# A fifth MLP pair's first two blocks ahead of the MLP, and three changes of order in layer 1's mixer and projection

## The chip, the cores and the metric

The kernel runs on one core of one Trainium2 chip. The metric is the device time of one execution in microseconds (us). Three runs of the kernel before took 2485.15, 2485.99 and 2488.28 us. A separate execution was profiled; every row shown here is from that one.

## What is computed

Two layers of a decoder trunk over 1024 positions of width 1024, in fp32. Layer 0 mixes with a gated DeltaNet, layer 1 with a state-space scan that ends in a gated linear unit (GLU). Beside the mixer, 4 heads of cross-attention read 256 memory tokens. Both outputs are concatenated (1536 rows), projected, added to the scaled input and normalised; an MLP with squared ReLU follows in the same way.

```
h = jnp.concatenate([mix, cross], axis=-1) @ w_o[i]
x = layer_norm(DN_ALPHA * x + h, ln1_g[i], ln1_b[i])
f = jnp.square(jax.nn.relu(x @ mlp_w1[i])) @ mlp_w2[i]
x = layer_norm(DN_ALPHA * x + f, ln2_g[i], ln2_b[i])
```

In layer 1, the mixer's last step is `out = zg * sigmoid(zg @ w_glu + b_glu)`.

## The kernel before

**Matmuls in three passes.** Every fp32 operand is split into a high part (a ScalarE cast to the type fp32r) and a low part (a VectorE subtraction). `mm3` (lines 386 to 391) multiplies high by high, high by low and low by high into one PSUM bank. Nearly all matmuls of the kernel come from these three lines; the tile's name tells the stage.

**Seven products for eight.** The large products use Strassen's scheme in Winograd's form: two by two blocks, seven block products numbered 1 to 7, and sums of blocks before and after. Product 1 is A11 B11 and product 2 A12 B21; both go to the first quarter of the output. Products 6, 7 and 4 are added onto the bank of product 1 (or 6), and 3 onto that of 5: this is what `onto` says.

**The GLU** (`glu`, lines 2094 to 2206). The weights w and the gated input z lie in SBUF as quarters, four row blocks each. The products go in the order 1, 5, 6, 3, 7, 4, 2, in two sets of four PSUM banks: set 0 (pa, pa, pa, sc) for 1, 6, 7, 4 and set 1 (mm, mm, pi, po) for 5, 3, 2. `sources` makes the sums in place; `t2`, product 4's factor, gets its last subtraction at the start of each of product 4's row blocks. When a product ends, each of its four banks is copied, added or gated by `gate`, which stores rows of the DRAM tensor cat. Product 4 gives rows 0 to 3 of the left half of the tokens, product 2 rows 4 to 7.

**The output projection** (`out_proj`, lines 1639 to 1677, and `out_seven`, lines 1679 to 1767). It has 12 row blocks of 128. Row blocks 8, 9, 10, 11, 0, 1, 2, 3 are paired as (8, 9), (10, 11), (0, 1), (2, 3) for the seven products, so each product loops over four row blocks j. Row block 4 is the fifth one, j = 4: it is added to products 3 and 4, and makes two small products of its own, 8 and 0, of one row block. Product 0 is its part of the output's first quarter, which products 1 and 2 fill. Products 1, 6, 7, 4, 8 are chain 0, and 2, 5, 3, 0 chain 1. In layer 1 chain 0 has the banks (mm, mm, pi, po) and chain 1 (pa, pa, pa, sc), and the order is 2, 1, 5, 6, 7, 4, 3, 8, 0; layer 0 has another order and other banks. After each product four additions on VectorE (lines 1759 and 1761) bring the banks into the rows y. Row blocks 5 to 7 follow as plain products in the tail (`acc_steps`, tile tm, banks pi, po, sc in turn), for one group of 128 positions (tau, 0 to 7) after the other.

**The end of a block** (`block_end`, lines 2390 to 2433). When a tau is complete, `done` normalises its rows, stores them and transposes them. The MLP's input is made into seven factors: "11" and "21" come from tau 0 to 3 alone, "22", "t1", "t2" and "t3" need tau 4 to 7 too, and "n4" comes last, in the four buffers of tag w1.

**Pairs ahead.** The MLP's first product has 16 pairs of hidden blocks, seven products each. Of pairs 0 to 3, products 1 and 2 are done ahead, in `mlp_ahead` (lines 615 to 624): it loads and splits 128x1024 weights (tag raw, two buffers, then tag w1, four), multiplies block 1 into a bank (pA), copies the result away (p1), adds block 2 onto the bank, and stores the first block of the hidden layer. Pairs 0, 1 and 2 are called at tau 5, 6 and 7, pair 3 after tau 7. In `mlp_first` (lines 761 to 772) these pairs do their products 5, 6, 7, 3 and 4 with weights whose sums were made long before (`mlp_weights`, line 642). All other pairs take all seven in `mlp_chain`, with weights summed on the spot (lines 650 to 674). In layer 0, pair 0 begins with ten filler matmuls (line 692) whose result is not used.

**The order.** Nothing runs in program order. `settle` (lines 58 to 293) takes all instructions behind the start-up, gives each a duration from a table (`price`) and a due time from the matmul that needs it, and lists them anew for every engine, DMA issues included. A matmul may be pulled forward by up to 40 us of due time; buffers of one tag are given out in the order of their first uses. The order is fixed at build time; on the chip each engine follows its list and waits where an operand is late.

Of the kernel before, what the change touches and what calls it, by code (L numbers as in the profile page):

```python
# [10 lines left out]
F32 = mybir.dt.float32  # L11
# [5 lines left out]
P = 128  # L17
# [3 lines left out]
HALF = 512  # L21
# [5 lines left out]
def f32(ap):  # L27
    return ap.bitcast(F32)


class Trunk:
# [570 lines left out]
    def hidden_sums(self, n, A11, A12, A21, A22):  # L602
# [7 lines left out]
        for b, o, x, z, op in ((3, A22, A21, A22, ALU.add), (5, A21, A11, A21, ALU.subtract),  # L610
                               (4, A11, A22, A11, ALU.subtract), (6, A12, A12, A11, ALU.subtract)):
            V.tensor_tensor(o, x, z, op=op)
            self.nc.sync.dma_start(self.hd[n, b], o)

    def mlp_ahead(self, i, n, B, ahead):

        w = self.load_split(self.a["w1"][i, 2 * n], "w1", "w1")
        a = self.psum("mm", "pA")
        self.block(a, [z[:, :HALF] for z in w], B["11"], True)
        p1 = self.tile("h3", [P, HALF], F32, "p1")  # L620
        self.nc.scalar.copy(p1, a)
        self.block(a, [z[:, HALF:] for z in w], B["21"], False)
        self.hidden(n, 0, a)
        ahead.append(p1)
# [13 lines left out]
    def mlp_weights(self, i, n, more):  # L638


        V = self.nc.vector
        if not more:
            s3, s1, A22 = (self.tile(t, [P, HALF], F32, "w1s") for t in ("h3", "h5", "h4"))
            self.nc.sync.dma_start(s1, self.wsum[i, n, 1][:, HALF:])
            r = self.load_raw(self.wsum[i, n, 0], "w1s")
            self.nc.sync.dma_start(s3, self.wsum[i, n, 1][:, :HALF])
            self.nc.sync.dma_start(A22, self.a["w1"][i, 2 * n + 1][:, HALF:])
            tags = iter(("h1", "h2") * 5)
            return {m: self.split(x, next(tags), "w" + str(m)) for m, x in ((5, s1), (6, r[:, :HALF]), (7, s3), (3, r[:, HALF:]), (4, A22))}
        r = self.load_raw(self.a["w1"][i, 2 * n], "w1r")  # L650
        A11, A12 = r[:, :HALF], r[:, HALF:]
        A21, A22 = (self.tile("h4", [P, HALF], F32, "w1r") for _ in range(2))
        for c, o in enumerate((A21, A22)):
            self.nc.sync.dma_start(o, self.a["w1"][i, 2 * n + 1][:, c * HALF:(c + 1) * HALF])
        new = lambda nm: self.tile("h3", [P, HALF], F32, nm)

        def sub(o, x, y):
            V.tensor_tensor(o, x, y, op=ALU.subtract)
            return o

        home = {1: 'h1', 2: 'h2', 6: 'h1', 5: 'h2', 7: 'h1', 3: 'h2', 4: 'h2'}
        ops = lambda m, s, nm: self.split(s, home[m], nm)
        s1 = new("s1")
        V.tensor_tensor(s1, A21, A22, op=ALU.add)
        s2 = sub(new("s2"), s1, A11)
        O = {}
        O[1] = ops(1, A11, "a1")
        O[2] = ops(2, A12, "a2")
        O[6] = ops(6, s2, "s2")
        O[5] = ops(5, s1, "s1")  # L670
        O[7] = ops(7, sub(new("s3"), A11, A21), "s3")
        O[3] = ops(3, sub(s2, A12, s2), "s4")
        O[4] = ops(4, A22, "a4")
        return O
# [1004 lines left out]
    def out_seven(self, i, y, early):  # L1679

        nc = self.nc
        V = nc.vector
        tt = lambda o, x, z, op: V.tensor_tensor(o, x, z, op=op)
        A_, S_ = ALU.add, ALU.subtract
        pairs = (8, 9), (10, 11), (0, 1), (2, 3)
        sets = [("mm", "mm", "pa", "pa")] * 2 if early else [("mm", "mm", "pi", "po"), ("pa", "pa", "pa", "sc")]
        w = self.a["w_o"][i]
        row = lambda k: self.cat[k * P:(k + 1) * P]
        L, R = slice(0, HALF), slice(HALF, 2 * HALF)
        tokens = (L, R) if early else (R, L)  # L1690
        ab, rq = [], []
        for c in range(2):
            for o in (ab, rq):
                o.append(self.tile("xT", [P, 8, HALF], F32, "os"))
            for n in range(8):
                p, j = (n % 2, n // 2) if c else (1 - n // 4, n % 4)
                nc.sync.dma_start(ab[-1][:, 4 * p + j], row(pairs[j][p])[:, tokens[c]])
                nc.sync.dma_start(rq[-1][:, 4 * p + j], w[pairs[j][p]][:, (L, R)[c]])
        spare = []

        def sources(m, j):
            if j == 4:
                out = []
                for src, c in ((row(4), tokens[m in (4, 8)]), (w[4], (L, R)[m in (3, 8)])):
                    out.append(self.tile("h3", [P, HALF], F32, "o4"))
                    nc.sync.dma_start(out[-1], src[:, c])
                return out
            aL, bL, aR, bR, rL, qL, rR, qR = (x[h][:, 4 * p + j] for x in (ab, rq) for h in range(2) for p in range(2))
            if m == (6 if early else 5):
                if j % 2 == 0:  # L1710
                    spare.append([self.tile("w1", [P, 2, HALF], F32, "os") for _ in range(2)])
                s1, t2 = (x[:, j % 2] for x in spare[j // 2])
                tt(s1, aR, bR, A_)
                tt(rL, rR, rL, S_)
            elif spare:
                s1, t2 = (x[:, j % 2] for x in spare[j // 2])
            if m == 6:
                tt(aR, aL, aR, S_)
                tt(t2, qR, rL, S_)
                tt(aL, s1, aL, S_)  # L1720
            if m == 7:
                tt(rR, qR, rR, S_)
                tt(bL, bL, aL, S_)
            if m == 4:
                tt(t2, qL, t2, S_)
            return {1: lambda: (aL, rL), 2: lambda: (bL, qL), 6: lambda: (aL, t2), 5: lambda: (s1, rL), 7: lambda: (aR, rR),
                    3: lambda: (bL, qR), 4: lambda: (bR, t2)}[m]()

        def operand(s, tag, nm):
            if isinstance(tag, str):  # L1730
                t = self.tile(tag, [P, 2, HALF], F32R, nm)
                hi, lo = t[:, 0], t[:, 1]
            else:
                hi, lo = (self.tile(t, [P, HALF], F32R, nm) for t in tag)
            nc.scalar.copy(hi, s)  # L1735
            tt(lo, s, f32(hi), S_)
            return hi, lo

        chain = {1: 0, 6: 0, 7: 0, 4: 0, 2: 1, 5: 1, 3: 1, 8: 0, 0: 1}
        into = {1: 0, 6: 1, 2: 0, 7: 3, 5: 3, 4: 2, 3: 1, 8: 3, 0: 0}  # L1740
        held, fresh = {}, {0, 1, 2, 3}
        for m in (2, 1, 6, 7, 4, 5, 3, 8, 0) if early else (2, 1, 5, 6, 7, 4, 3, 8, 0):
            onto = m in (6, 7, 4, 3)
            if not onto:
                held[chain[m]] = [self.psum(t, f"o{m}") for t in sets[chain[m]]]
            bank = held[chain[m]]
            items = {0: (4,), 8: (4,), 3: range(5), 4: range(5)}.get(m, range(4))
            for j in items:
                left, right = sources(m, j)
                h = operand(left, "raw", "ok")  # L1750
                x = operand(right, "w1" if m in (5, 3, 8, 0) else ("h2", "h2"), "ow")
                for t in range(4):
                    c = slice(t * P, (t + 1) * P)
                    self.mm3(bank[t], (h[0][:, c], h[1][:, c]), x, j == items[0] and not onto, j == items[-1], onto)
                    if j == items[-1]:
                        n = into[m]
                        o = y[4 * (n // 2 if early else 1 - n // 2) + t][n % 2]
                        if n in fresh:
                            V.scalar_tensor_tensor(o, o, ALPHA, bank[t], op0=ALU.mult, op1=ALU.add)
                        else:  # L1760
                            tt(o, bank[t], o, A_)
                    yield self.STEP
            fresh.discard(into[m])
            if m == 4:
                yield "early"
            if m == (5 if early else 4):
                yield "late"
# [326 lines left out]
    def glu(self):  # L2094
# [37 lines left out]
        def sources(m, j):  # L2132
# [14 lines left out]
            if m == 3:  # L2147
                tt(s, bL, aL, op=S_)
                tt(rL, qR, rR, op=S_)
            if m == 4:  # L2150
                tt(t2, qL, t2, op=S_)
            return {1: lambda: (aL, rL), 5: lambda: (s, rL), 6: lambda: (aL, t2), 3: lambda: (s, qR),
                    7: lambda: (aR, rL), 4: lambda: (bR, t2), 2: lambda: (bL, qL)}[m]()
# [25 lines left out]

        sets = ("pa", "pa", "pa", "sc"), ("mm", "mm", "pi", "po")  # L2180
        held = {}
        for m in (1, 5, 6, 3, 7, 4, 2):
            own, onto = int(m in (5, 3, 2)), m in (6, 7, 4, 3)
            if not onto:
                held[own] = [self.psum(t, f"g{m}") for t in sets[own]]
# [204 lines left out]
    def block_end(self, i, y, xd):  # L2390
# [3 lines left out]
        B, ahead = {}, []  # L2394

        def done(tau):
# [28 lines left out]
            fill("t3", a)  # L2425
            V.tensor_tensor(c, c, t2, op=ALU.subtract)
            if tau == 7:
                self.mlp_ahead(i, 3, B, ahead)
                B["n4"] = self.x_parts("w1")
                for n in range(4):  # L2430
                    self.parts(as4(y[n][1]), self.x_cols(B["n4"], n))

        return self.out_proj(i, y, done, i == 0), B, ahead

    def mlp_block(self, i, B, ahead, xd, side, out, more):
# [112 lines left out]
```

## Time and profile before

| what | value |
|---|---|
| median of 3 runs | 2485.99 us |
| profiled execution, its own time | 2487.54 us |
| its span, first to last instruction | 2485.8 us |
| TensorE matmuls | 12541, busy 99% of the span |
| VectorE (DVE) | busy 79% |
| ScalarE (ACT) | busy 57% |
| DMA, HBM read and written | 170 GB/s over the span |

In a timeline row stand the start, the duration, the engine, the line, the operation, the tile written and those read, the shape, and in square brackets how long the engine was idle before it and who released it. A matmul's duration of 0.39 us includes its passage through the array; the next starts before it ends. The stretches that matter: layer 0's block end is 741 to 800 us, layer 1's GLU 1640 to 1726, its projection 1726 to 1814, its tail and block end 1814 to 1881, and its pairs from then on.

### The profile page before, as it was taken

What the parts mean: (1) busy time and instruction counts of PE and PEld (TensorE: products, weight loads), DVE (VectorE), ACT (ScalarE), POOL (GpSimd) and SP (SyncE); (2) the same over time, 40 slices, a digit from 0 to 9 for tenths busy, and PEclk for the clock granted to TensorE, in tenths of its full rate; (3) what the DMA queues carried; (4) which work ended last, traced back from release to release, by engine and by line L of the source; (5) the groups of instructions that cost most, each with busy time, mean ns of one, the idle gap of its engine ahead of it and who ended that gap; (6) DMA issues with size and microseconds to landing.
All of it is one profiled execution on the core that took longest, in us unless ns stands there. A gap on an engine that the chain in (4) does not pass through costs nothing.

```text
span 2485.8 us, 37137 instructions
## 1 busy us (share of the span) xinstructions
PE 2452.7 (99%) x12541; PEld 2035.3 (82%) x12541; DVE 1960.5 (79%) x3688; ACT 1404.6 (57%) x3134; POOL 224.8 (9%) x333
## 2 busy tenths in 40 slices
PE   9999999999999999999999999999999999999998
PEld 7888888887787888788888888888877888888886
DVE  7776867685889987879988956698997665588777
ACT  6766767665557576554445244666465555544443
POOL 1111212111001011312220000000010000000001
PEclk9999999999999999999999999999999999999999
DMA  6444445456335665587455488685136544673422
GB/s 205 130 115 147 132 149 148 150 162 199 128 114 184 212 221 191 178 276 248 144 164 158 149 229 237 165 276 194 58 138 229 184 151 153 213 274 99 148 89 98
DMA packets 297807, 425.02 MB, mean 171 GB/s; under 512 B 105312, under 2 KB 141104, under 8 KB 297616
## 3 DMA queue, kind: packets, MB, share of 16 engines
q1 hardware_dynamic: 284912, 392.43, 49.6%
q0 software_dynamic: 10112, 25.64, 3.3%
q10 hardware_dynamic: 2592, 4.59, 0.5%
q8 instruction: 98, 1.61, 0.3%
q14 instruction: 93, 0.76, 0.1%
HBM read 286.79 MB, written 135.76 MB: 170 GB/s over the span
## 4 chain that ended last, share of the span: by engine, by line
PE 85%; DVE 7%; DMA 3%; issue 2%; ACT 2%; SPq 0%; POOL 0%; DVEq 0%; ACTq 0%; POOLq 0%
PE q L389 7%; PE q L390 7%; PE q L391 7%; PE pB L389 4%; PE pB L391 4%; PE pB L390 4%; PE wi L389 3%; PE wi L391 3%; PE wi L390 3%; PE o L389 2%; PE pC L391 2%; PE o L390 2%; PE o L391 2%; PE pC L390 2%; PE pC L389 2%
## 5 line engine op out<-in xcount | busy, mean ns | idle before, releaser
L389 PE MATMUL q<-wkh,hkh 128*128 128x512 f32 x784 | 306.0, 390 | 0.0
L390 PE MATMUL q<-wkl,hkh 128*128 128x512 f32 x784 | 305.7, 390 | 0.0
L391 PE MATMUL q<-wkh,hkl 128*128 128x512 f32 x784 | 305.3, 389 | 0.0
L857 ACT CAST wkh<-wr 128x512 fp32r<-128x512 f32 x168 | 104.8, 624 | 238.7 <-PE q L390 156.9
L389 PEld LDWEIGHTS q<-wkh,hkh 128*128 128x128 f32 x784 | 147.2, 188 | 31.7 <-ACT wkh L857 1.0
L391 PEld LDWEIGHTS q<-wkh,hkl 128*128 128x128 f32 x784 | 147.2, 188 | 30.6
L390 PEld LDWEIGHTS q<-wkl,hkh 128*128 128x128 f32 x784 | 147.2, 188 | 29.9
L858 DVE TENSOR_TENSOR wkl<-wr,wkh 128x512 fp32r<-128x512 f32 x168 | 115.7, 689 | 62.9 <-issue 49.7
L389 PE MATMUL wi<-xTh,wih 128*128 128x512 f32 x376 | 152.3, 405 | 1.8 <-ACT wih L368 1.8
L390 PE MATMUL wi<-xTl,wih 128*128 128x512 f32 x376 | 150.4, 400 | 0.0
L391 PE MATMUL wi<-xTh,wil 128*128 128x512 f32 x376 | 150.2, 400 | 0.0
L512 POOL TENSOR_TENSOR mv<-mv,mhalf 128x1 f32<-128x1 f32 x32 | 31.6, 988 | 1222.9 <-DVE mv L506 1111.1
L858 DVE TENSOR_TENSOR hkl<-hr,hkh 128x512 fp32r<-128x512 f32 x196 | 134.2, 684 | 4.4 <-ACT hkh L857 4.3
L857 ACT CAST hkh<-hr 128x512 fp32r<-128x512 f32 x196 | 120.8, 616 | 4.6 <-DMA hr<-hd 4.6
L389 PE MATMUL o<-ow,ok 128*128 128x512 f32 x256 | 101.4, 396 | 1.0 <-ACT ok L1735 1.0
L391 PE MATMUL o<-ow,ok 128*128 128x512 f32 x256 | 101.4, 396 | 0.1
L390 PE MATMUL o<-ow,ok 128*128 128x512 f32 x256 | 100.1, 391 | 0.1
L850 DVE TENSOR_TENSOR y<-q,y 128x512 f32<-128x512 f32 x136 | 88.0, 682 | 0.0
L389 PEld LDWEIGHTS wi<-xTh,wih 128*128 128x128 f32 x376 | 71.4, 190 | 15.4 <-ACT wih L368 2.0
L391 PEld LDWEIGHTS wi<-xTh,wil 128*128 128x128 f32 x376 | 71.3, 190 | 14.2 <-DVE wil L369 0.8
L390 PEld LDWEIGHTS wi<-xTl,wih 128*128 128x128 f32 x376 | 71.6, 190 | 12.6
L1735 ACT CAST ok<-os 128x512 fp32r<-128x512 f32 x56 | 34.6, 620 | 49.7 <-PE o L391 36.6
(627 smaller groups left out, 7254.2 us busy)
## 6 DMA issues: line engine op xcount, KB each, us to landing
hr<-hd SPq DMA_DIRECT2D x212, 256.0 KB, 2.7
wr<-in_w_dram SPq DMA_DIRECT2D x56, 512.0 KB, 5.7
hd<-u SPq DMA_DIRECT2D x100, 256.0 KB, 2.3
w1r<-in_w_dram SPq DMA_DIRECT2D x48, 512.0 KB, 3.8
hd<-hid SPq DMA_DIRECT2D x60, 256.0 KB, 2.1
hd<-p SPq DMA_DIRECT2D x60, 256.0 KB, 2.3
w1r<-in_w_dram SPq DMA_DIRECT2D x48, 256.0 KB, 3.3
wir<-in_w_in_dram SPq DMA_DIRECT2D x23, 512.0 KB, 3.8
```

Source lines behind the costliest of these rows:

```text
L389: mm(ps, a[0], b[0], start=start, stop=False, skip_group_check=onto)
L390: mm(ps, a[0], b[1], start=False, stop=False, skip_group_check=onto)
L391: mm(ps, a[1], b[0], start=False, stop=stop, skip_group_check=onto)
L512: nc.gpsimd.tensor_tensor(mv[:, 3:4], mv[:, 2:3], self.mhalf[:, 0:1], op=ALU.pow)
L850: V.tensor_tensor(o, bank[t], o, op=ALU.add)
L857: nc.scalar.copy(hi, s)
L858: nc.vector.tensor_tensor(lo, s, f32(hi), op=ALU.subtract)
L1735: nc.scalar.copy(hi, s)
```

## The change

Four edits. A table `AHEAD` says how many pairs are begun ahead in each layer, five in both, and the fifth is called behind the fourth, before "n4"; its copy p1 has a buffer of tag h2 in layer 0 and h5 in layer 1, and pair 4 no longer splits weights 1 and 2 and takes the short form of the pairs ahead. In layer 1's projection product 1 goes before product 2, product 2 gets row block 4 as a fifth one, and product 0 goes. In the GLU, products 4 and 2 change places, and `t2`'s last subtraction moves to product 7.

```
+    AHEAD = (5, 5)
+
     def mlp_ahead(self, i, n, B, ahead):
...
-        p1 = self.tile("h3", [P, HALF], F32, "p1")
+        p1 = self.tile(("h2", "h5")[i] if n > 3 else "h3", [P, HALF], F32, "p1")
...
+        half = n < self.AHEAD[i]
...
-        O[1] = ops(1, A11, "a1")
-        O[2] = ops(2, A12, "a2")
+        if not half:
+            O[1] = ops(1, A11, "a1")
+            O[2] = ops(2, A12, "a2")
...
-        for m in (2, 1, 6, 7, 4, 5, 3, 8, 0) if early else (2, 1, 5, 6, 7, 4, 3, 8, 0):
+        for m in (2, 1, 6, 7, 4, 5, 3, 8, 0) if early else (1, 2, 5, 6, 7, 4, 3, 8):
...
-            items = {0: (4,), 8: (4,), 3: range(5), 4: range(5)}.get(m, range(4))
+            items = {0: (4,), 8: (4,), 2: range(4 if early else 5), 3: range(5), 4: range(5)}.get(m, range(4))
...
-            if m == 4:
+            if m == 7:
                 tt(t2, qL, t2, op=S_)
...
-        for m in (1, 5, 6, 3, 7, 4, 2):
+        for m in (1, 5, 6, 3, 7, 2, 4):
...
-                self.mlp_ahead(i, 3, B, ahead)
+                for n in range(3, self.AHEAD[i]):
+                    self.mlp_ahead(i, n, B, ahead)
```

## Rows read from the trace of the kernel before

**Rows 1.** The page's first part: busy time of each engine.
```profile
PE 2452.7 (99%) x12541; PEld 2035.3 (82%) x12541; DVE 1960.5 (79%) x3688; ACT 1404.6 (57%) x3134; POOL 224.8 (9%) x333
```

**Rows 2.** Timeline of TensorE, projection into tail: twelve matmuls in a full stretch.
```profile
1812.30 0.39 PE L389 MATMUL o<-ow,ok 128*128 128x512 f32 x1
...
1814.80 0.39 PE L391 MATMUL tm<-ow,oc 128*128 128x512 f32 x1
```

**Rows 3.** Busy time by stretch: stretch, length, each engine, clock, DMA.
```profile
760.00:800.00 40.00, 38.72 (x187) 30.79 (x186) 39.47 (x73) 31.70 (x70) 6.08 (x6) 1.00 0.56 180
...
1740.00:1800.00 60.00, 59.98 (x262) 48.71 (x261) 60.00 (x100) 28.70 (x50) 0.00 (x0) 1.00 0.14 52
...
1860.00:1890.00 30.00, 26.87 (x123) 20.81 (x122) 29.12 (x53) 22.91 (x47) 2.06 (x2) 1.00 0.69 223
1890.00:1905.00 15.00, 13.75 (x61) 11.02 (x60) 9.14 (x15) 7.98 (x14) 0.00 (x0) 1.00 0.73 239
```

**Rows 4.** Timeline of TensorE at the end of layer 1's block.
```profile
1873.23 0.63 PE L531 MATMUL xt<-ident,y 128*128 128x128 f32 x4 [0.71 <-DVE y L519]
...
1875.29 0.40 PE L391 MATMUL pA<-xB,w1l 128*128 128x512 f32 x1
1876.36 0.50 PE L389 MATMUL pA<-xB,w1h 128*128 128x512 f32 x1 [0.68 <-ACT p L621]
...
1879.44 0.39 PE L390 MATMUL pC<-xB,w5h 128*128 128x512 f32 x1
1880.57 0.49 PE L389 MATMUL pB<-xB,w6h 128*128 128x512 f32 x1 [0.74 <-ACT xB L540]
1881.61 0.50 PE L391 MATMUL pC<-xB,w5l 128*128 128x512 f32 x1 [0.54 <-DVE w5l L586]
```

**Rows 5.** Timeline of TensorE in layer 1's third pair.
```profile
1901.46 0.39 PE L390 MATMUL pB<-xB,w6h 128*128 128x512 f32 x1
1903.10 0.50 PE L391 MATMUL pC<-xB,w5l 128*128 128x512 f32 x1 [1.25 <-DVE w5l L586]
```

**Rows 6.** Timeline of VectorE at the same place.
```profile
1900.18 0.69 DVE L586 TENSOR_TENSOR w6l<-w1s,w6h 128x512 fp32r<-128x512 f32 x1 [1.90 <-ACT w6h L585]
...
1902.36 0.69 DVE L586 TENSOR_TENSOR w5l<-w1s,w5h 128x512 fp32r<-128x512 f32 x1
```

**Rows 7.** Timeline of VectorE, layer 1: the fourth pair's split, pair 0's w5l.
```profile
1866.57 1.22 DVE L369 TENSOR_TENSOR w1l<-w1r,w1h 128x1024 fp32r<-128x1024 f32 x1
...
1880.87 0.69 DVE L586 TENSOR_TENSOR w5l<-w1s,w5h 128x512 fp32r<-128x512 f32 x1
```

**Rows 8.** The page's DMA issues: operation, count, KB each, us to landing.
```profile
w1r<-in_w_dram SPq DMA_DIRECT2D x48, 512.0 KB, 3.8
```

**Rows 9.** Timeline of SyncE's DMA queue, layer 1: raw loads of pairs 0 and 1.
```profile
1864.89 0.32 SPq L359 DMA_DIRECT2D w1s<-wsum  x1
...
1867.82 0.32 SPq L359 DMA_DIRECT2D w1s<-wsum  x1
```

**Rows 10.** Timeline of TensorE at the end of layer 0's block.
```profile
792.37 0.40 PE L391 MATMUL pA<-xB,w1l 128*128 128x512 f32 x1
793.38 0.93 PE L692 MATMUL pB<-xB,w6h 128*128 128x512 f32 x3 [0.61 <-DVE tw L2419]
```

**Rows 11.** VectorE's groups by line, 1726 to 1814 us: count, busy us, mean ns.
```profile
L1683 DVE TENSOR_TENSOR y<-o,y 128x512 f32<-128x512 f32 x17 | 10.9, 681 | 0.0
L1759 DVE SCALAR_TENSOR_TENSOR y<-y,o 128x512 f32<-128x512 f32 x16 | 10.4, 678 | 0.0
```

**Rows 12.** Timeline of TensorE in the projection.
```profile
1782.21 0.39 PE L391 MATMUL o<-ow,ok 128*128 128x512 f32 x1
1782.61 0.50 PE L389 MATMUL o<-ow,ok 128*128 128x512 f32 x1
```

## Prediction, before the change was run

> **What bounds the kernel.** I read the page's busy list first [rows 1]. TensorE counts as busy for 2452.7 us of a span of 2485.8 us; VectorE comes second with 79%. That busy time hides small holes, because matmuls overlap, so I went on to the times at which neighbouring matmuls start. In a full stretch eleven steps take 2.50 us, 0.227 us for one 128x512 matmul [rows 2]. A hole is what a step takes above 0.227 us, and it costs time however the busy column looks. The table by stretch [rows 3] says where to search: in layer 1 the projection from 1740 to 1800 us has TensorE at 59.98 of 60 us, while VectorE has no idle time at all; the end of the block, 1860 to 1905 us, has TensorE at 40.6 of 45 us. Layer 0's end, 760 to 800 us, has 38.72 of 40. So the change can only win at the two ends of the attention blocks, and the projection must not lose what it has.
>
> **What stands at the end of layer 1.** The starts there [rows 4] give these holes: 1875.29 to 1876.36 is 1.07, so 0.84 us, waiting for ScalarE to copy the last ready pair's product 1; 1879.44 to 1880.57 is 1.13, so 0.90 us; 1880.57 to 1881.61 is 1.04, so 0.81 us. Together 2.55 us. At the last two TensorE has started pair 0 and takes each operand as it arrives: a factor (xB) that ScalarE cast late, and a weight's low half (w5l) that VectorE made late. The transposes of the last rows wait as well, 0.71 us for VectorE's normalisation. Later, 1901.46 to 1903.10 is 1.64, so 1.41 us [rows 5]. That one is another kind: VectorE works in a fixed order, and pair 2's w5l stands behind pair 3's w6l, which waited 1.90 us for its cast [rows 6].
>
> **The edits, one by one.**
>
> *Fifth pair ahead, layer 1.* Blocks 1 and 2 are 2 x 4 x 3 = 24 matmuls, 24 x 0.227 = 5.45 us. They are moved, not added: pair 4 loses them from its own chain. They need only the two factors from the first four row groups, which are complete long before 1875 us, so they can stand where TensorE waits. The work in front of them on VectorE is one 128x1024 subtraction, 1.22 us [rows 7], which has to be done in a stretch where VectorE is 29.12 of 30 us busy [rows 3]. It pushes everything of pair 0 back by at most that; w5l, done at 1881.6 [rows 7], would come at 1882.8. TensorE, with the three holes filled, comes to pair 0 about 5.45 - 0.84 = 4.6 us after 1879.2, at 1883.8, about 1 us after its operands. I therefore count all 2.55 us as won; bounds 0 (if the order written at build time puts the new blocks elsewhere) and 3.3 us (if the transposes' 0.71 goes too). I leave the 0.71 standing: the planner puts a transpose first as soon as it believes the rows ready, whatever other work there is.
>
> Its DMA: one more 512 KB load, which takes 3.8 us from issue to landing [rows 8], and a 256 KB reload of the finished first block for the sums. The load takes one of two "raw" buffers. Before, pair 0 and pair 1 got theirs at 1864.89 and 1867.82 [rows 9], just after the splits of the third and fourth pair ahead. Now the fifth takes the first of these places, pair 0 gets 1867.82, and pair 1 waits for the fifth's split. That needs the w1 buffers of the third pair, whose blocks end shortly before the fourth's first one at 1875.29 [rows 4]: some 7 us later than before. Pair 1's w6 is wanted only after pair 0's blocks 5, 6, 7 and its own 5, 4 x 12 x 0.227 = 10.9 us, so I price the delay at nothing; without that cover it would be up to 4 us. Behind it in SyncE's order stand stores and prefetches that nobody waits for soon. No load of the change goes through POOL's queue. The fourth factor n4 takes all four w1 buffers and so comes after the fifth pair's blocks too; pair 0's product 4 wants it five blocks on, 13.6 us. The new buffer for the copy, one of nine h2 in layer 0 and of five h5 in layer 1, leaves the weights of the pairs a little less room; by itself I give that no price.
>
> The same pair later leaves the chained form: VectorE does two 128x512 additions more there and its two small splits go, ScalarE does two copies fewer. An instruction costs VectorE 60.00 / 100 = 0.60 us [rows 3], so this nets to zero beside the matmuls.
>
> *The hole at 1903.* TensorE now comes 5.45 - 2.55 = 2.9 us later to this place, and w5l would still be done around 1903, or 1 to 2 us later for the delayed loads. It is filled if the order holds, and an order can turn. I take half, 0.7 us; bounds -1 (it grows) and +1.4.
>
> *Fifth pair ahead, layer 0.* Here ten filler matmuls (L692) stand in the waits, and they stay. What is left is 792.37 to 793.38, 1.01, so 0.78 us [rows 10], where the filler waits for VectorE to read the bank of the last transposes. The fifth pair's first block is free work at that place. I take 0.8 us; bounds 0 and 1.3.
>
> *Row block 4 into product 2.* The 12 matmuls of product 0 become matmuls of product 2, none goes. Four VectorE additions go, 4 x 0.60 = 2.4 us; y<-o,y is 0.68 us each as the trace's list has it [rows 11]. TensorE is full beside them, so they bring nothing directly. At the end of the projection product 8 now comes last, and its four banks include two that the following tail products (tm) use first. They were empty for 12 matmuls before; now each must be drained just in time. I price that at 0.3 us lost; bounds 0 and 1.5 (one drain and its queue).
>
> *Product 1 before product 2, and GLU's swap.* These belong together: GLU now ends in the bank set that product 2 uses, and product 1 starts in the other. Left-token rows 0 to 3 are written last, some 11 us later than before; product 5 is the first to read them, after 48 + 60 matmuls, 24.5 us. The four subtractions moved into GLU's product 7 lie beside 48 matmuls. Nothing here waits now and I price it at zero, with one exception.
>
> *Product 5 directly behind product 2, on the same four banks.* Before, product 1 stood between. The first bank is finished 9 matmuls, 2.04 us, before product 5 wants it, and one drain takes 0.68 us [rows 11]: about 1.2 us of slack, if VectorE is on time. Products 6 and 7 already follow each other on one bank set, and where product 4 follows 7, at its fourth bank by the count of matmuls, the hole is 0.17 us [rows 12]. By that row the handover costs nothing, and that is what I take. The Trainium skill says the opposite in Perfetto Trace Analysis, Optimizing Tensor Performance: independent matmul groups should rotate through different PSUM banks so that draining one overlaps the next. Taken fully, four drains would be exposed here and four before the tail, 8 x 0.68 = 5.4 us, and the sum below would turn into a loss of 1.4 us.
>
> **The sum.** Won 2.55 + 0.7 + 0.8 = 4.05, lost 0.3: 3.75 us. The profiled execution took 2487.54 us, 1.55 us above the median of the three runs, 2485.99. So 2483.8 against its own time, and 2482.2 as a median. About 0.2%, 5 us, is what a measurement of this kernel tells from no change.
>
> **Rivals.** *A, the forecast* (47%): 2480.5 to 2484.
>
> *B, the holes only move* (22%). The whole instruction order is planned at build time from estimated durations, so each hole above is an estimate that came out short, and VectorE stays the engine behind them. The program's own order, which the edits change, is a wish that the planner may overrule: it may also put the blocks where they were. For it: VectorE at 97% from 1860 to 1890, and the waits for one operand at a time. Against it: 5.45 us of work that waits for none of this. Gain 0 to 1.5, 2485.3.
>
> *C, more than the holes counted* (15%). The lighter VectorE also closes the transposes' waits and the small handovers: 3.3 + 1.4 + 1.3 = 6.0, 2480.0.
>
> *D, the projection loses VectorE's lead* (16%), slower. Per row block VectorE has 4, 5 and 4 instructions in products 5, 6 and 7, and 4 additions per product: 20, 24 and 20 x 0.60 = 12.0, 14.4 and 12.0 us beside 48 matmuls of 10.9 us. It falls behind by 1.1 + 3.5 + 1.1 = 5.7 us and lives from the lead that it builds in the first two products. If the tight drains between 2 and 5, or the late rows 0 to 3, hold VectorE up there by more than its lead, that deficit shows on TensorE, with the 2.4 us of drains: 8.1 - 4.05 = 4 us slower, 2490.0. It decides once VectorE is over 1.2 us late at the end of product 2. Against it: four additions go from this stretch, and the longer product 2 lets it gain 13.6 - 8.4 = 5.2 instead of 3.7 us. The skill's rule on banks is one part of this case.
>
> **Chances and range.** Faster by over 0.2% means below 2481.0: a quarter of A and most of C, 0.25. Slower means above 2491.0: the upper half of D and what I have not seen, 0.09. The rest, 0.66, is within. The range 2478.5 to 2489.5 leaves out the end of C and half of D.
>
> **What would show it.** In layer 1's end, pair 4's blocks (pA<-xB) should stand before the first pC<-xB,w5, with no wait there for the casts and w5l; the stretch of 45 us should have under 2 us of holes. In layer 0 the filler should follow more pA work. Between 1740 and 1815 TensorE must stay full, with 32 y drains in place of 36. The forecast is wrong if holes appear at the first matmuls of product 5 or of the tail, or if pair 1 waits for its raw load.

## The result, and the profile after

The changed kernel takes 2490.76 us (median of 21 runs; 21 runs of the kernel before on the same chip: 2485.99). The ratio is 1.0018, with a 95% interval of 1.0011 to 1.0024: **slower by 4.5 us** (2.7 to 6.0), where 3.75 us faster was forecast. The profiled execution took 2490.98 us, its span is 2489.3 us, 3.5 us more than before.

The busy list of the page hardly differs from [rows 1].

```profile
PE 2453.0 (99%) x12541; PEld 2036.1 (82%) x12541; DVE 1958.4 (79%) x3686; ACT 1403.1 (56%) x3128; POOL 218.4 (9%) x333
```

The table by stretch does. Columns as in [rows 3]: stretch, length, busy time of TensorE, weight load, VectorE, ScalarE and GpSimd, granted clock, DMA share, GB/s. First the kernel after, at the ends of the blocks and in the projection, which answer to [rows 3], and in one more stretch of layer 0:

```profile
760.00:800.00 40.00, 39.15 (x190) 31.35 (x189) 39.56 (x72) 31.22 (x69) 6.03 (x6) 1.00 0.55 179
...
930.00:950.00 20.00, 18.72 (x83) 15.17 (x82) 16.60 (x43) 14.71 (x27) 6.13 (x12) 1.00 0.67 239
...
1740.00:1800.00 60.00, 60.00 (x266) 49.58 (x265) 59.41 (x98) 28.69 (x50) 0.00 (x0) 1.00 0.24 78
...
1860.00:1890.00 30.00, 28.83 (x136) 22.48 (x135) 29.56 (x51) 23.77 (x49) 2.51 (x2) 1.00 0.61 201
1890.00:1905.00 15.00, 15.00 (x67) 12.18 (x66) 12.67 (x25) 9.99 (x21) 0.00 (x0) 1.00 0.77 271
```

From 1860 to 1905 us TensorE was busy for 26.87 + 13.75 = 40.62 us, and is now for 28.83 + 15.00 = 43.83: 3.2 us less idle. Some of it is lost again in the stretch in front, layer 1's tail, where the changed kernel has new waits. That stretch in the kernel before and then in the one after:

```profile
1814.00:1860.00 46.00, 45.85 (x223) 36.72 (x222) 44.22 (x86) 34.93 (x86) 6.78 (x7) 1.00 0.42 149
```

```profile
1814.00:1860.00 46.00, 45.26 (x216) 36.16 (x215) 40.32 (x77) 30.85 (x75) 6.33 (x6) 1.00 0.34 121
```

From 1814 to 1905 us TensorE was busy for 45.85 + 40.62 = 86.47 us and is now for 45.26 + 43.83 = 89.09, so 2.6 us is won at this end. In layer 0, 760 to 800 us, 0.43 us is won. The projection has 60.00 of 60. New is the hole in 930 to 950, where the kernel before was full (its row stands under layer 0's part, among the experiments).

Now the stretch between GLU and projection, in the kernel before and then in the one after:

```profile
1720.00:1725.00 5.00, 5.00 (x24) 4.14 (x23) 3.88 (x6) 2.28 (x4) 0.00 (x0) 1.00 1.08 369
1725.00:1731.00 6.00, 6.00 (x29) 4.95 (x28) 6.00 (x11) 4.79 (x8) 0.00 (x0) 1.00 1.04 372
1731.00:1740.00 9.00, 9.00 (x41) 7.48 (x40) 8.33 (x15) 4.98 (x9) 0.00 (x0) 1.00 0.92 296
```

```profile
1720.00:1725.00 5.00, 5.00 (x24) 4.14 (x23) 3.31 (x6) 1.76 (x3) 0.00 (x0) 1.00 1.06 398
1725.00:1731.00 6.00, 1.81 (x7) 0.99 (x6) 1.54 (x3) 0.97 (x2) 0.00 (x0) 0.84 1.06 377
1731.00:1740.00 9.00, 9.00 (x31) 7.21 (x31) 8.48 (x15) 6.63 (x13) 0.00 (x0) 0.73 0.27 84
```

Here is the loss, and it has two parts. The timeline of TensorE after shows both:

```profile
1725.40 0.39 PE L391 MATMUL g<-gx,gk 128*128 128x512 f32 x1
1725.63 0.39 PE L389 MATMUL o<-ow,ok 128*128 128x512 f32 x1
1730.21 0.79 PE L390 MATMUL o<-ow,ok 128*128 128x512 f32 x1 [4.19 <-DVE ow L1687]
...
1731.40 0.63 PE L389 MATMUL o<-ow,ok 128*128 128x512 f32 x1
1731.83 0.63 PE L390 MATMUL o<-ow,ok 128*128 128x512 f32 x1
...
1735.67 0.49 PE L390 MATMUL o<-ow,ok 128*128 128x512 f32 x1
1736.00 0.40 PE L391 MATMUL o<-ow,ok 128*128 128x512 f32 x1
```

**The hole.** The second matmul of the projection comes 4.58 us after the first. Less one step of 0.227 us [rows 2] that is 4.35 us lost. **The clock.** Behind the hole the steps are 0.427 us (the first two 0.60), nearly twice the full stretch's. The granted clock says the same: 0.84 over 6 us and 0.73 over 9 us is (6 x 0.16 + 9 x 0.27) / 0.5 = 6.8 us at the lower level, 1.2 GHz in place of 2.4. The steps are full again at 1736.00, so about 1 us of it lies in the hole itself. From 1730.21 to 1736.00 stand 13 steps in 5.79 us; at 0.227 they take 2.95, so this costs 2.84 us more. Together 7.2 us. With 1.28 us lost at 942 and 2.6 and 0.43 won at the blocks' ends the parts make 5.4 us, where the span grew by 3.5; where the other 1.9 us were won isn't shown.

What TensorE waited for: the low half of the first row block's weights. VectorE was to make it, and stood still for 6 us with nothing else done. Its timeline, with the first of the four results `go` of product 2 ahead of it:

```profile
1717.18 0.68 DVE L2181 TENSOR_TENSOR go<-go,gz 128x512 f32<-128x512 f32 x1
...
1722.03 1.28 DVE L1687 TENSOR_TENSOR os<-os 128x512 f32<-128x512 f32 x2
1729.46 0.69 DVE L1687 TENSOR_TENSOR ow<-os,ow 128x512 fp32r<-128x512 f32 x1 [6.14 <-DMA cat<-go]
```

The one who released it is a store, of the GLU's result `go` to cat. VectorE doesn't read what is stored; it writes `ow`, and `go` and `ow` are both tiles of tag h2. The table `keep` in the GLU puts the first output quarter, copied at the end of product 1, into four h2 buffers; product 2 completes it, and each buffer is free only when its store has landed. Before, product 2 was the GLU's last; now it is the last but one, and the order written at build time gives its buffers to the projection's first weights. ScalarE stood still as long, before the cast of the next row block's weights, which goes into an h2 buffer too:

```profile
1730.03 0.62 ACT L1739 CAST ow<-os 128x512 fp32r<-128x512 f32 x1 [6.30 <-DMA zz<-yd]
```

The profile puts that wait down to a load; why the cast had to wait for it isn't shown. TensorE would have stood at this cast next: it is 12 matmuls from 1725.63 to the next row block, so it wanted it at about 1728.4.

The chain of waits tells the rest (start, length, what):

```profile
1712.28 5.74 DMA os<-cat
...
1718.04 5.36 DMA os<-in_w_o_dram
...
1723.45 5.88 DMA cat<-go
...
1729.46 0.70 DVE ow L1687
...
1730.21 0.79 PE o L390
```

The first `go` was ready at 1717.9 and the last at 1721.5. The first of the four stores was issued at 1723.45, 5.6 us after its rows were ready, behind loads on SyncE's list, and then took 5.88 us to land. By estimate from these numbers, issued when its rows were ready and just as slow, it would have landed at 1723.7, VectorE would have been done at about 1724.5, and TensorE wants the result at 1725.9. By that the place on the list counts as much as the landing. No run tests a store that is issued earlier. The Trainium skill, in Perfetto Trace Analysis, Summary: the profiler window per engine type, says that the interval shown for a DMA on an engine's queue leaves out the movement of the data. The trace agrees: the store counts 0.32 us on SyncE, and its buffer came free 5.88 us after its start. In the kernel after, the stores of tile `go` (from issue to landing, min, median, max), first the eight issued from 1695 to 1711 us, then the four of product 2:

```profile
DMA to landing us min/median/max: 2.0/2.0/2.5
```

```profile
DMA to landing us min/median/max: 5.1/5.5/5.8
```

### The profile page after: what moved, and what is told of

Its sections match the earlier page's. It is cut to its first block, busy times and chain, and to the rows that moved or that the text cites. A ratio compares the mean times of both kernels' runs of the same rounds, so it can differ in the third digit from the quotient of the medians.

```text
span 2489.3 us, 37135 instructions
## 1 busy us (share of the span) xinstructions
PE 2453.0 (99%) x12541; PEld 2036.1 (82%) x12541; DVE 1958.4 (79%) x3686; ACT 1403.1 (56%) x3128; POOL 218.4 (9%) x333
## 4 chain that ended last, share of the span: by engine, by line
PE 86%; DVE 6%; DMA 3%; issue 2%; ACT 2%; POOL 0%; SPq 0%; DVEq 0%; ACTq 0%; POOLq 0%
PE q L389 7%; PE q L390 7%; PE q L391 7%; PE pB L389 4%; PE pB L390 4%; PE pB L391 4%; PE wi L389 3%; PE wi L391 3%; PE wi L390 3%; PE pC L390 2%; PE pC L391 2%; PE pC L389 2%; PE o L390 2%; PE o L391 2%; PE o L389 2%
```

## The experiments

Ratios are to the kernel before, with 95% intervals.

**Which half of the change costs?** e1_ahead_only keeps the fifth pair and takes back the three edits of order; e2_mixer_only does the reverse.

```
e1:
-        for m in (2, 1, 6, 7, 4, 5, 3, 8, 0) if early else (1, 2, 5, 6, 7, 4, 3, 8):
+        for m in (2, 1, 6, 7, 4, 5, 3, 8, 0) if early else (2, 1, 5, 6, 7, 4, 3, 8, 0):
-            items = {0: (4,), 8: (4,), 2: range(4 if early else 5), 3: range(5), 4: range(5)}.get(m, range(4))
+            items = {0: (4,), 8: (4,), 3: range(5), 4: range(5)}.get(m, range(4))
-            if m == 7:
+            if m == 4:
-        for m in (1, 5, 6, 3, 7, 2, 4):
+        for m in (1, 5, 6, 3, 7, 4, 2):
e2:
-    AHEAD = (5, 5)
+    AHEAD = (4, 4)
```

> Fifth pair ahead in both layers, GLU and projection in the order of before. Buffer theory (the loss is at the GLU's handover alone, from a buffer of tag h2 that is held by a late store): no hole at 1726 us, the block ends win what the changed kernel's trace shows there, 0.7 + 0.4 us in layer 0 and 1.2 + 1.6 us in layer 1, less the new 1.4 us hole near 941: 2483.0 us. Rival (the fifth pair's loads or buffers push the handover too): over 2486.

> Four pairs ahead as before; GLU's swap, product 1 first and row block 4 in product 2 as changed. Buffer theory and load theory alike: the hole of 4.35 us and the halved clock behind it, 7.2 us together, stand alone: 2493.2 us. If the hole needs the fifth pair, 2486.

e1: ratio 0.9986 (0.9977 to 0.9995), 3.5 us faster. e2: 1.0029 (1.0019 to 1.0039), 7.2 us slower. The two together make +3.7 us, against 4.5 measured for the whole change. So the loss lies in the edits of order alone, and the fifth pair wins, 1.2 to 5.7 us by the interval. The stretch at the end of layer 1 in e1:

```profile
1860.00:1905.00 45.00, 43.85 (x198) 34.85 (x197) 40.01 (x70) 33.76 (x68) 2.51 (x2) 1.00 0.73 232
```

It is as in the changed kernel (43.83), and at 1726 us e1 has no hole.

**Is it the buffer?** Two ways to take the h2 buffers out of the store's hands. e3_keep_swapped exchanges the tags of two quarters; e8_keep_gb puts the first quarter into the two whole-row buffers of tag gb. The order of the products stays as changed.

```
e3:
-        keep = {0: ["h2"] * 4, 1: ["h1"] * 3 + ["h4"], 3: ["h1"] * 4}
+        keep = {0: ["h1"] * 4, 1: ["h1"] * 3 + ["h4"], 3: ["h2"] * 4}
e8:
-                        o[q, t] = self.tile(keep[q][t], [P, HALF], F32, "go")
+                        if q == 0:
+                            if t % 2 == 0:
+                                both = self.tile("gb", [P, T], F32, "go")
+                            o[q, t] = both[:, (t % 2) * HALF:(t % 2 + 1) * HALF]
+                        else:
+                            o[q, t] = self.tile(keep[q][t], [P, HALF], F32, "go")
```

> The changed kernel, but the GLU's first quarter (product 2's results) is kept in buffers of tag h1 and its fourth quarter (product 7's) in h2. Nothing else is touched. Buffer theory: the projection's low parts no longer wait for the store of product 2's rows; no hole, the clock stays up: 2490.8 - 7.2 = 2483.6 us. Load theory (the first product's rows and weights land late because the DMA engines are full): the hole stays, 2490.8.

> The changed kernel, but product 1's and 2's GLU quarter is kept in two tiles of tag gb, which stand empty then, in place of four of tag h2; the other quarters stay where they are. Buffer theory: no hole at 1726 us and none at 1672 (which came from taking h2 for another quarter), the clock stays up: about 7 us faster than the changed kernel, 2.5 to 3.5 us faster than before. Load theory: the hole stays, 4 to 5 us slower than before.

e3: 0.9999 (0.9991 to 1.0008), 4.7 us faster than the changed kernel where 7.2 was expected. The hole at 1726 and the low clock are gone, but h2 is now taken by the fourth quarter from the middle of the GLU on, and the timeline of TensorE there shows a new hole, in product 6, for the cast of a right operand:

```profile
1674.22 0.50 PE L389 MATMUL g<-gx,gk 128*128 128x512 f32 x1 [1.71 <-ACT gx L2165]
```

e8: 0.9987 (0.9978 to 0.9996), as expected. The same stretches as above are full, at the full clock:

```profile
1725.00:1731.00 6.00, 6.00 (x29) 4.95 (x28) 6.00 (x11) 5.18 (x10) 0.00 (x0) 1.00 1.09 370
1731.00:1740.00 9.00, 9.00 (x41) 7.48 (x40) 9.00 (x16) 2.92 (x6) 0.00 (x0) 1.00 0.50 159
```

The place of one quarter is worth 1.0018 - 0.9987 = 0.0031, 7.7 us, within some 3 us by the two intervals; the hole and the clock came to 7.2 in the trace. DMA is as full here as in the changed kernel (share 1.09), so at this place a busy DMA by itself delayed nobody: it took someone who waits for a store. ScalarE's wait of 6.30 us is gone too.

**Each edit of order alone.** e4_merge_only (fifth row block into product 2, products 2 and 1 in their old order) and e5_glu_only (only GLU's exchange); both without the fifth pair.

```
e4:
-    AHEAD = (5, 5)
+    AHEAD = (4, 4)
-        for m in (2, 1, 6, 7, 4, 5, 3, 8, 0) if early else (1, 2, 5, 6, 7, 4, 3, 8):
+        for m in (2, 1, 6, 7, 4, 5, 3, 8, 0) if early else (2, 1, 5, 6, 7, 4, 3, 8):
-            if m == 7:
+            if m == 4:
-        for m in (1, 5, 6, 3, 7, 2, 4):
+        for m in (1, 5, 6, 3, 7, 4, 2):
e5: AHEAD as in e4, and the first two pairs of lines of e1
```

> Four pairs ahead and the GLU as before; in layer 1's projection only row block 4 goes into product 2 and product 0 goes, with product 2 still first. Buffer theory: no hole at the start, since product 2's GLU rows are not waited for: 2486.0. The rival on banks and VectorE's lead (drains at the tail's start are exposed): 0.3 to 1.5 us slower, 2486.3 to 2487.5.

> Only the GLU's last two products change places (with t2's subtraction); the projection and the four pairs ahead as before, so the projection's product 2 follows the GLU's product 4 on the same four banks. Buffer theory: product 2's rows are stored among the loads, a DVE wait for that store stands at the projection's first products, 3 to 6 us slower than before. Bank theory (a handover on one bank set exposes the drains): TensorE waits for ScalarE's gates in PSUM instead, 1 to 2.7 us. Neither: same time as before.

Each alone costs as much as the three edits together (e2, 1.0029), as far as the intervals tell: e4 1.0038 (1.0025 to 1.0052), which I had not expected, e5 1.0035 (1.0022 to 1.0049). Of e4's five times three are 2500.3 to 2501.2 us and two 2493.9 and 2494.9; the profiled execution is the latter, so some 5 us of e4's median stands in no trace. In e4 the same wait comes later, on VectorE's timeline: the fifth row block's weights take h2 buffers (product 0 had taken them from w1), which product 2's results of the GLU still hold.

```profile
1737.15 0.69 DVE L1687 TENSOR_TENSOR ow<-os,ow 128x512 fp32r<-128x512 f32 x1 [5.12 <-DMA cat<-go]
```

In e5 it comes earlier, inside the GLU's last product, whose right operands (gx) are h2 tiles too. The timelines of ScalarE and of TensorE:

```profile
1728.82 0.62 ACT L2165 CAST gx<-gs 128x512 fp32r<-128x512 f32 x1 [8.59 <-DMA cat<-go]
```

```profile
1731.23 0.79 PE L389 MATMUL g<-gx,gk 128*128 128x512 f32 x1 [6.26 <-ACT gk L2165]
```

TensorE's releaser there is a cast that only stood in line behind the one that waited.

**The same two with the buffer elsewhere.** e10_merge_gb is e4 and e11_glu_gb is e5, each with the lines of e8. As a control, e13_before_gb is the kernel before with these lines alone.

> The run with row block 4 merged into product 2 (e4), and the GLU's first quarter kept in two whole-row buffers instead of four h2 buffers, nothing else changed. Buffer theory: the fifth row block's weight halves need h2 buffers that the quarter's results held until stored; with them elsewhere the holes of 1734 to 1745 and the halved clock go, ratio to before 1.000 plus or minus 0.001 (some 2486 us by the first median of before). Rival, that five row blocks in product 2 are too many for VectorE or for the banks: holes near 1735 stay, ratio near 1.004.

> The run with GLU's last two products exchanged alone (e5), and the first quarter kept in two whole-row buffers. Buffer theory: the last product's right halves take h2 buffers too, which the quarter's results held in e5; the hole of 6.4 us at 1724 and the halved clock go, ratio to before between 0.999 and 1.001. Rival, the exchange itself (the gate's work too late in the last product, or the stores queued behind the projection's loads on SP): a hole of over 2 us stays between 1720 and 1735, ratio 1.002 or more.

> The kernel before with the first quarter kept in whole-row buffers alone, as a control. Buffer theory: in the kernel before nothing waits for those h2 buffers, so nothing is won: ratio 0.9995 to 1.0005. If it is under 0.999, the whole-row buffers bring a gain of their own, and the gain of the runs that use them is not a sign of the buffer theory.

e11: 0.9993 (0.9983 to 1.0002), the hole and the low clock are gone: against e5 the buffer alone is worth 1.0035 - 0.9993 = 0.0042, 10 us, within some 4. The control: 1.0005 (0.9996 to 1.0014), so the gb buffers bring nothing of their own. e10: 1.0012 (1.0003 to 1.0021), outside what was expected: some two thirds of e4's loss by the medians are gone and the rest stays, for which the buffer theory has no room. Its rest is a wait of another kind. The timelines of ScalarE and of TensorE in e10:

```profile
1737.18 0.62 ACT L1739 CAST ok<-os 128x512 fp32r<-128x512 f32 x1 [2.10 <-PE o L391]
1737.71 0.61 ACT L1739 CAST ow<-o 128x512 fp32r<-128x512 f32 x1
```

```profile
1738.37 1.02 PE L389 MATMUL o<-ow,ok 128*128 128x512 f32 x2 [1.23 <-ACT ow L1739]
```

The fifth row block's weight stands on ScalarE behind the left operand of the next row block, which waits 2.10 us for TensorE to free its raw buffer. Behind this hole and a second wait of 0.39 us the clock fell as well, 0.83 over 10 us or 3.4 us at the lower level:

```profile
1740.00:1750.00 10.00, 10.00 (x38) 8.09 (x38) 8.70 (x15) 3.43 (x6) 0.00 (x0) 0.83 0.79 290
```

e4 has the same wait of 1.23 us, at 1744.20, beside that for the store. In the changed kernel, product 1 first, TensorE has no such hole; why the order came out so in e10 was not tried.

**Layer 0's part, and the remaining mixes.** e6_ahead_l1 is e1 with the fifth pair in layer 1 alone (`AHEAD = (4, 5)`); e12_ahead_l1_mixer_gb is e8 with the same; e9_ahead_gb_oldorder is e1 with the lines of e8.

> Fifth pair ahead in layer 1 alone, everything else as before. If the gain is layer 1's holes at the block end and in the third pair, about 2.8 us faster than before, nearly the whole of what both layers win together (3.5 us); layer 0's share is then under 1 us, because a new hole of 1.4 us near 941 us takes back what the block end wins. If layer 0 carries the gain, under 1.5 us faster.

> The changed kernel with the first quarter in whole-row buffers and the fifth pair's two blocks ahead in layer 1 alone. By the holes of the trace, layer 0's part takes away 1.1 us before 850 and gives back 1.4 us at 941; so this one should be level with the run that has both layers ahead (ratio 0.9987), between 0.998 and 0.9995. If layer 0's part pays, it is over 1 us slower than that run; if it costs, over 0.5 us faster.

> Fifth pair ahead in both layers, GLU and projection in the order of before, and the same quarter in gb. There is no hole at the handover to close in this order, so the time of the fifth pair alone: 3.5 us faster than before, within 1 us. If h2 is short in other places of that stretch too, 4.5 or more.

e6 0.9992 (0.9983 to 1.0001), e12 0.9992 (0.9984 to 1.0001), e9 0.9992 (0.9983 to 1.0). That is 2.0 us faster, where 2.8 was expected of e6 and 3.5 of e9; e12 lies where it was expected. By time none of them differs from e1 and e8, so time doesn't tell what layer 0's part is worth. By place it can be told: the stretch 930 to 950 in the kernel before and then in e6 is full,

```profile
930.00:950.00 20.00, 20.00 (x89) 16.46 (x89) 19.21 (x46) 15.14 (x28) 7.74 (x14) 1.00 0.77 263
```

```profile
930.00:950.00 20.00, 20.00 (x89) 16.49 (x89) 19.04 (x45) 15.12 (x28) 8.06 (x15) 1.00 0.78 270
```

while the kernel after has 18.72 and this wait on TensorE's timeline, for ScalarE's work on a hidden block:

```profile
942.54 0.50 PE L389 MATMUL pB<-xB,s3h 128*128 128x512 f32 x1 [1.28 <-ACT u L738]
```

So layer 0's part wins 0.43 us at the block's end in the changed kernel and nothing in e1 (38.71 us busy from 760 to 800, 38.72 before), and loses 1.28 us at 942.

The best by the median are e8 and e1, about 3.3 us under the kernel before. The intervals of both leave out a ratio of 1, narrowly; e1, e6, e8, e9 and e12 can't be told apart.

## Why the prediction was wrong

**The step that failed** is "Product 1 before product 2, and GLU's swap": "Nothing here waits now and I price it at zero". In its place came a hole of 4.35 us at product 1's first row block and 2.84 us of lower clock, 7.2 us. e2 gives 7.2 us for it together with row block 4 in product 2; no run has this step without that one, but the GLU's exchange alone (e5) costs 8.7 us, at another place. I followed the data: which bank a product uses, when rows 0 to 3 are written, who reads them. I did not follow the buffers: which tag the results lie in, until when, and who takes that tag next. The code says it in one line, `keep`, and the two users in `operand`. "Row block 4 into product 2" has the same fault: priced at 0.3 us, at most 1.5, it costs some 9 us alone (e4), and in the changed kernel only the foreseen wait at the tail:

```profile
1820.32 0.50 PE L389 MATMUL tm<-ow,oc 128*128 128x512 f32 x1 [0.19 <-DVE y L1687]
```

**The price of a store** was read in the wrong place. I had 3.8 us for a load from the page's list over the whole execution [rows 8], and saw the DMA from 1740 on, where its share is 0.14 [rows 3]. The kernel before already had a full DMA at 1720 to 1731, 1.08 and 1.04 in the rows above, and its list of DMA issues from 1715 to 1735 us (operation, count, KB each, median us to landing) has a store (cat<-sig) and a load (y<-x) that are as slow as the stores that hurt after:

```profile
cat<-sig SPq DMA_DIRECT2D x4, 256.0 KB, 5.0
...
y<-x SPq DMA_DIRECT2D x3, 256.0 KB, 5.9
```

After, in the same stretch:

```profile
os<-in_w_o_dram SPq DMA_DIRECT2D x6, 256.0 KB, 5.4
cat<-go SPq DMA_DIRECT2D x4, 256.0 KB, 5.5
```

Loads and stores take the same 5 to 6 us there. A buffer that waits for a store in this stretch could have been priced from the trace of before.

**The clock** had no term. Before, this place had no drop, and I asked of each wait only how long it is. Here 4.35 us of wait cost 2.84 us more.

**What was right.** *Layer 1's end*: 2.55 + 0.7 = 3.25 us forecast, 89.09 - 86.47 = 2.6 measured. Pair 4's blocks stand ahead of nearly all of pair 0's, the three holes of [rows 4] and that of [rows 5] are gone, the last one whole and not by half. That the sums come close is in part luck, since new waits in the tail took some of it back. Left standing, as foreseen, is the transposes' wait; a smaller one for a factor's cast remains:

```profile
1880.04 0.63 PE L531 MATMUL xt<-ident,y 128*128 128x128 f32 x4 [0.72 <-DVE y L519]
...
1888.40 0.50 PE L389 MATMUL pB<-xB,w6h 128*128 128x512 f32 x1 [0.45 <-ACT xB L540]
```

*Layer 0*: 0.8 us forecast; 0.43 was won there, and the wait at 942 takes it back, which I had not looked for. The whole of the fifth pair is 3.5 us in e1 and 2.0 in e9, against 4.05 in the sum; the intervals, e1's from 1.2 to 5.7, hold both.

*The handover from product 2 to product 5*: zero, and zero it is, 60.00 of 60. The rule of the Trainium skill (Perfetto Trace Analysis, Optimizing Tensor Performance) that independent matmul groups should rotate through different PSUM banks doesn't speak against it as I had taken it to: each product goes through four banks in turn. The trace shows no exposed drain at this place.

*The rivals.* The time came out 0.8 us above D's 2490.0, but D is not what happened: VectorE has idle time in the projection (59.41 of 60), and the only late drain is the 0.19 us at the tail. D's loss was to come at products 5 to 7; the true one came at the first matmuls of product 1, and none of my signs of failure named that place. That the time lies near D's is luck.

## What to carry to other kernels

When products change places, list for every buffer tag that they touch who holds it, until which event, and who takes it next; where the holder's end is a store, the buffer comes free at the store's landing. Price that landing in its own stretch, not by the median over the execution, and count what stands before the store on its queue. Where a new wait falls on TensorE, look in the granted clock for what it costs behind it.

## What the runs showed of the hardware

In the kernel after, stores of 256 KB took 2.0 to 2.5 us to land when issued from 1695 to 1711 us, and 5.1 to 5.8 when issued from 1723 to 1726, where the DMA moved 377 to 398 GB/s. A hole of 4.35 us in TensorE's work went with 6.8 us at the lower clock, which cost 2.84 us more. How long a single wait is didn't decide it: in e10 waits of 1.23 and 0.39 us close together were followed by 3.4 us at the lower level, while the hole of 1.41 us at 1901 in the kernel before [rows 5] stood in a stretch with a granted clock of 1.00 [rows 3], and so did e3's wait of 1.71 us:

```profile
1660.00:1690.00 30.00, 27.95 (x120) 22.49 (x121) 24.01 (x39) 14.74 (x27) 0.00 (x0) 1.00 0.55 193
```
